# Queries and keys projected transposed and stored as the operands of the attention's scores

## The chip, the cores and the metric

The kernel runs on one core of a Trainium2 chip. The metric is the device time of one execution in microseconds (us); the time of a kernel is the median of its runs. The engines of the core are named as in the profile: PE (TensorE, matrix products; PEld is its weight load), DVE (VectorE), ACT (ScalarE), POOL (GpSimd) and SP (SyncE, which here does nothing but start transfers). Data lie in 128 partitions of SBUF; matrix products are accumulated in PSUM, which has eight banks of 128 x 512 fp32 values. All five engines take their instructions in order, each from its own queue, and wait for one another by semaphores.

## The reference

One layer of a hybrid decoder, in fp32, for a prompt of 1024 rows of width 1024 and for eight samples that each decode one token over a paged cache of 8192 tokens. What matters here is the first part, for the prompt:

```python
def rmsnorm(x, g):
    xf = x.astype(jnp.float32)
    y = xf * lax.rsqrt(jnp.mean(xf * xf, axis=-1, keepdims=True) + EPS)
    return (y * g.astype(jnp.float32)).astype(x.dtype)
...
    h = xn @ w_in
    q = h[..., O_Q:O_K].reshape(B, T, ATT_HEADS, ATT_HEAD_DIM)
    k = h[..., O_K:O_V].reshape(B, T, ATT_HEADS, ATT_HEAD_DIM)
    v = h[..., O_V:O_F].reshape(B, T, ATT_HEADS, ATT_HEAD_DIM)
    logf = jax.nn.log_sigmoid((h[..., O_F:O_U] + b_f).astype(jnp.float32))
    u = jax.nn.gelu(h[..., O_U:O_Z])
    z = rmsnorm(jax.nn.gelu(h[..., O_Z:]), g_sgu_v).reshape(B, T, SGU_HEADS, SGU_HEAD_DIM)
...
    s = jnp.einsum('bqhd,bkhd->bhqk', q, k).astype(jnp.float32) * (ATT_HEAD_DIM ** -0.5)
    s = s + (cq.astype(jnp.float32).transpose(0, 2, 1)[:, :, :, None]
             - ck.astype(jnp.float32).transpose(0, 2, 1)[:, :, None, :])
    s = jnp.where(kpos[None, :] <= qpos[:, None], s, -jnp.inf)
    p = jax.nn.softmax(s, axis=-1).astype(v.dtype)
    return jnp.einsum('bhqk,bkhd->bqhd', p, v)
```

There are eight heads of 64 columns; `cq` and `ck` are running sums of `logf` over the tokens. Queries, keys and values of the prompt are 512 columns each, and keys and values are outputs as well. The rest is a gating group beside the attention, an output projection, cross-attention into 256 memory tokens, a gated MLP with a convolution over the rows, and a final norm; the samples go through the same with their own caches.

## The kernel before

**Products.** A large product is fp32 made of three products of halves: an operand is split into a high part (an fp32r copy, on ACT) and a low part (what is left, on DVE or POOL; `split`, L212), and `gemm3` (L246) adds high by high, high by low and low by high in PSUM. 1/rms of a row is not multiplied into x. It is put on at the evacuation of PSUM, as a scale of one value to a partition (`rstd`; for queries `rstd8`, an eighth of it), since a partition of the result is a token.

**Buffers.** U are 18 buffers of 128 x 1024, of which x transposed takes 16 (high and low, 8 blocks each) during the projections; T2 are seven of 128 x 520; KV four of 128 x 2048 (the cache's tiles and the rows of x); `wr`, `wh`, `wl` are four, five and four buffers of a weight piece as loaded, its high and its low part. PSUM has four banks `ba`, two `bb`, one `ms`, one `dv`; `BK()` takes `ba` and `bb` in turn, two to one.

**What sets the order.** The kernel is written as generators. The prompt's main one runs through the stages and yields an estimate of its PE time at many points; a driver (L1640 to L1660) then lets the background, the samples' decode over the paged cache, take a step whenever enough has gathered (`PACE`). The framework fixes the order of instructions on each engine and the slots of the buffers when the kernel is built, with the order in the program as priority; on the chip each engine follows its order, and an instruction waits for what it reads and for the slot that it writes. Transfers of SP and ACT share eight semaphore lanes that go round; a transfer also waits for the one that had its lane before.

**The projections, `p1` (L309 to L537).** Column groups in the order queries, forget logits with u, keys, values, z; 9 to 278 us of the profiled execution. For each group four pieces of `w_in` are loaded and split (`loaded`), and the samples' own small products are made from the unsplit weights (`sample_mm`, L262; summed by `sample_sum`, L276). Then for each of eight blocks of 128 tokens the block of x is the stationary operand and 512 columns of weights move (`mm_chunk`, and `by_rows` at L402 to L404 for four blocks at once, which lets the first products start as the pieces come in): eight blocks of the contraction by three products, 24 matmuls of 128 x 512. `evac` (L389 to L393) puts each result through ACT with its scale into a T2 buffer and stores it from ACT's queue: queries to a scratch `q_d`, keys and values to the outputs `o_k` and `o_v`, all with a token to a row. `stats` (L331 to L342), called for each half of 512 rows, loads the rows of x by SP behind all pieces of x transposed (`x_in`), sums their squares on ACT (L207), and makes 1/rms on DVE (L200), POOL (L201) and DVE (L341, L342).

**The attention (L638 to L828), once for each half of 512 query rows.** It goes over four pairs of heads, in each over two blocks of 256 rows, two heads and two blocks of 128 rows. `load` fetches the pair's queries, keys and values (three transfers from SP, L644 to L651). `setup` transposes queries and keys on PE (L657, L680), four blocks to a bank, and writes the operands of the scores: for each head `qq`, which has the high part of the queries in partitions 0 to 63 and the low part in 64 to 127 (copies L663, L664 on ACT, subtract L665 on DVE); `ka`, the high part of the keys twice, one above the other (L684 on ACT; L688 on ACT in the first half, L686 on POOL in the second); `kb`, the low part (L689 on DVE). Four rows of the running sums are loaded beside them from POOL's queue. With these, two matmuls give the scores of a block in full accuracy (`scores`, L704 and L706), to which a causal mask is added on the diagonal. DVE takes the maximum (L709), ACT the exponential (L714); `turn` transposes the probabilities (L732) and ACT or DVE copies them (L739); `values` multiplies (L748); a closing step normalizes. Turns and values follow the scores two blocks behind. The next pair is loaded at the point `LD` and set up at the point `ST`, spread over yields, in the midst of the pair before. The memory's key and value projections (`pmem`) and, in the background, the decode's steps run among these.

## Time and profile before

| | |
|---|---|
| median of 3 runs | 1987.51 us (1987.01 to 1988.8) |
| the profiled execution | 1999.7 us, its span 1997.9 us |
| mean granted clock of PE | 0.958 |
| projections of queries | 9 to 60 us |
| forget logits with u | 60 to 118 us |
| keys | 118 to 175 us |
| values, then z | 175 to 278 us |
| attention of both halves | 278 to 545 us: PE busy 224.7 of 267, DVE 181.6, ACT 172.1, POOL 94.6, clock 0.91 |
| all that follows | 545 to 1998 us: PE busy 1352 of 1452 |

Busy times of an engine are given beside the length of the stretch, in us; a granted clock of 1.00 is the full one and 0.50 half. A line such as `PE ba L704 <- ACT u L688` means that PE, about to write a `ba` bank at line 704, waited for ACT to finish the tile `u` at line 688. Line numbers are those of the kernel before unless a text says otherwise.

### The profile page before, as it was taken

The page shows a single profiled execution, that of the slowest core. Times are in us where ns is not written, and L with a number is a line of the kernel's source. Part 1 is how long each engine was busy: PE and PEld are TensorE (multiplying, and loading weights), DVE is VectorE, ACT ScalarE, POOL GpSimd, SP SyncE. Part 2 cuts the span into 40 slices and gives each one's busy share as a digit, 9 for nine tenths or more (in the row PEclk, how much of TensorE's full clock was granted, in tenths as well). Part 3 has the DMA queues.
Part 4 walks back from the last instruction along what each step waited for, and adds up shares of the span by engine and source line. Part 5 has one row for each costly group of instructions (what it writes and reads, how often), then busy time and mean ns, then how long its engine had stood idle before and what let it go on. Part 6 is the DMA issues. An engine that isn't in the chain of part 4 may idle for free.

```text
span 1997.9 us, 24107 instructions
## 1 busy us (share of the span) xinstructions
PE 1838.5 (92%) x9159; PEld 1300.7 (65%) x9159; DVE 1332.5 (67%) x1467; ACT 732.9 (37%) x1344; POOL 988.4 (49%) x560
## 2 busy tenths in 40 slices
PE   8899989778999697999999999789999999899997
PEld 5777766556667455676777667566566668567773
DVE  3877456677677988998879999885424439532232
ACT  5332246566632322332323323322424423232331
POOL 1664343433387547676767576557243344233321
PEclk9999989889999898899999999899999999899999
DMA  8766786754497888888878889878664458666755
GB/s 322 258 235 229 270 318 229 251 172 154 165 356 263 306 296 311 297 309 312 313 279 329 292 296 336 328 259 306 259 225 162 141 192 268 239 197 224 258 204 191
DMA packets 160467, 517.05 MB, mean 259 GB/s; under 512 B 20168, under 2 KB 41928, under 8 KB 127584
## 3 DMA queue, kind: packets, MB, share of 16 engines
q0 software_dynamic: 38528, 270.88, 36.3%
q1 hardware_dynamic: 114912, 232.06, 33.6%
q10 hardware_dynamic: 6912, 12.59, 1.7%
q8 instruction: 72, 1.18, 0.2%
q14 instruction: 43, 0.35, 0.1%
HBM read 493.63 MB, written 21.84 MB: 258 GB/s over the span
## 4 chain that ended last, share of the span: by engine, by line
PE 65%; DVE 18%; DMA 6%; issue 5%; ACT 3%; POOL 2%; SPq 0%; POOLq 0%; ACTq 0%; DVEq 0%
PE ba L250 11%; PE ba L252 11%; PE ba L251 11%; PE bb L250 5%; PE bb L251 5%; PE bb L252 5%; DVE kv L1191 4%; PE dv L1250 4%; DVE s L1195 4%; DMA kv<-cache_k,kidx 2%; POOL wl L216 1%; DVE kv L1414 1%; PE dv L1493 1%; DMA kv<-cache_v,kidx 1%; PE ba L1022 1%
## 5 line engine op out<-in xcount | busy, mean ns | idle before, releaser
L216 POOL TENSOR_TENSOR wl<-wr,wh 128x1024 fp32r<-128x1024 f32 (+1 forms) x184 | 450.0, 2456 | 358.5 <-PE ba L252 211.6
L215 ACT ACTIVATE wh<-wr 128x1024 fp32r<-128x1024 f32 (+2 forms) x220 | 228.1, 1042 | 398.9 <-PE ba L251 105.1
L1191 DVE TENSOR_TENSOR kv<-kv,d 128x2048 f32<-128x2048 f32 (+1 forms) x109 | 308.7, 2836 | 42.6 <-DMA kv<-cache_k,kidx 42.4
L1183 POOL DMA_INDIRECT kv<-cache_k,kidx x128 | 175.8, 1373 | 287.4 <-PE dv L1250 110.3
L1195 DVE TENSOR_REDUCE s<-kv 128x32 f32<-128x2048 f32 (+1 forms) x139 | 292.1, 2107 | 29.4 <-POOL kv L1191 28.2
L1244 POOL DMA_INDIRECT kv<-cache_v,kidx x128 | 184.5, 1441 | 206.7 <-PE dv L1250 96.5
L250 PE MATMUL ba<-wh,u 128*128 128x512 f32 (+1 forms) x674 | 261.9, 390 | 7.1 <-ACT u L215 6.0
L251 PE MATMUL ba<-wl,u 128*128 128x512 f32 (+1 forms) x674 | 258.5, 384 | 1.3 <-DVE wl L216 1.3
L252 PE MATMUL ba<-wh,u 128*128 128x512 f32 (+1 forms) x674 | 257.6, 383 | 0.0
L250 PE MATMUL ba<-u,wh 128*128 128x512 f32 x568 | 231.3, 408 | 0.6 <-DVE u L219 0.5
L252 PE MATMUL ba<-u,wl 128*128 128x512 f32 x568 | 227.2, 401 | 0.0
L251 PE MATMUL ba<-u,wh 128*128 128x512 f32 x568 | 227.2, 400 | 0.0
L250 PEld LDWEIGHTS ba<-wh,u 128*128 128x128 f32 x674 | 128.1, 190 | 52.3 <-issue 17.8
L252 PEld LDWEIGHTS ba<-wh,u 128*128 128x128 f32 x674 | 127.8, 190 | 33.1 <-issue 7.5
L251 PEld LDWEIGHTS ba<-wl,u 128*128 128x128 f32 x674 | 128.2, 190 | 31.7 <-issue 6.5
L1250 PE MATMUL dv<-kv,s 128*32 128x512 f32 x1024 | 137.6, 627 | 5.5 <-DMA kv<-cache_v,kidx 5.5
L250 PEld LDWEIGHTS ba<-u,wh 128*128 128x128 f32 x568 | 108.9, 192 | 49.2 <-issue 14.3
L1191 POOL TENSOR_TENSOR kv<-kv,d 128x2048 f32<-128x2048 f32 (+1 forms) x30 | 117.0, 3908 | 43.9 <-DMA kv<-cache_k,kidx 38.7
L252 PEld LDWEIGHTS ba<-u,wl 128*128 128x128 f32 x568 | 108.5, 191 | 32.8 <-issue 7.6
L251 PEld LDWEIGHTS ba<-u,wh 128*128 128x128 f32 x568 | 108.7, 191 | 31.0 <-issue 5.9
L250 PE MATMUL bb<-wh,u 128*128 128x512 f32 (+1 forms) x318 | 125.5, 395 | 3.1 <-ACT u L215 1.5
L251 PE MATMUL bb<-wl,u 128*128 128x512 f32 (+1 forms) x318 | 123.3, 388 | 2.1 <-DVE wl L216 2.1
(395 smaller groups left out, 3079.1 us busy)
## 6 DMA issues: line engine op xcount, KB each, us to landing
wr<-w_up SPq DMA_DIRECT2D x88, 512.0 KB
kv<-w_up SPq DMA_DIRECT2D x22, 1024.0 KB
wr<-w_down SPq DMA_DIRECT2D x40, 512.0 KB
kv<-w_down SPq DMA_DIRECT2D x11, 1024.0 KB
wr<-w_in SPq DMA_DIRECT2D x16, 512.0 KB
wr<-w_o SPq DMA_DIRECT2D x16, 512.0 KB
wr<-w_cq SPq DMA_DIRECT2D x16, 512.0 KB
wr<-w_co SPq DMA_DIRECT2D x16, 512.0 KB
```

The costliest lines, as they stand in the source:

```text
L215: nc.scalar.activation(h, src, AF.Copy)
L216: (eng or nc.vector).tensor_tensor(l, src, h.bitcast(F32), op=ALU.subtract)
L250: mmul(out, sh, mh, start=(i == 0), stop=False)
L251: mmul(out, sh, ml, start=False, stop=False)
L252: mmul(out, sl, mh, start=False, stop=(i == n - 1))
L1022: mmul(ps, mv[:, mt, dd * P : (dd + 1) * P], pT[:, mt, :], start=(mt == 0), stop=(mt == 1))
L1183: nc.gpsimd.indirect_dma_start(kv, None, a["cache_k"], off(kidx[:, b, ch : ch + 1]))
L1191: eng.tensor_tensor(kvv[:, i : i + m, :], kvv[:, i : i + m, :], qb.unsqueeze(1).broadcast_to((P, m, 512)), op=ALU.mult)
L1195: nc.vector.tensor_reduce(s[:, ch * 4 + i : ch * 4 + i + m, :].rearrange("p k h -> p (k h)"), kvv[:, i : i + m, :].rearrange("p k (h d) -> ...
L1244: nc.gpsimd.indirect_dma_start(kv, None, a["cache_v"], off(kidx[:, b, ch : ch + 1]))
L1250: mmul(dv[32 * j : 32 * j + 32, :], s[:, ch * 4 : ch * 4 + 4, :].rearrange("p k h -> p (k h)"), kvv[:, j, :], start=(ch == 0), stop=(ch == ...
L1414: nc.vector.tensor_tensor(kn, kn, qb[n].unsqueeze(1).broadcast_to((P, 2, 512)), op=ALU.mult)
```

## The change

In the projections of queries and keys the operands trade places: a block of 128 weight columns (two heads) is stationary and 512 tokens of x move, so that a result has a head's column to a partition and a token to a column. There are as many matmuls of the same size. Values, u, z and the forget logits stay as they were. 1/rms now lies along the columns, so `stats` spreads it: `dg` is the identity times the four columns of `rstd`, and a product with ones gives every partition the whole row, which ACT copies to `rrow`, a further U buffer (lines 341 to 350 of the changed kernel). The first projection, `by_cols`, does four column blocks of the first 512 tokens at once. `evac_T` multiplies by scale and `rrow` on DVE, splits the result (a copy on ACT, a subtract on DVE), and stores high and low part each to a scratch of shape 512 x 1024 from ACT's queue; keys are also stored, unsplit, from SP to the output, which is transposed now and turned on the host. In the attention, `setup` and its point `ST` are gone, and so are its five yields per pair; `load` fetches the operands as they are used, three pieces of queries and three of keys per head and one of values per pair, 13 transfers from SP in place of three, into buffers that are all taken at the point `LD`. In the first half values now lie in a T2 buffer.

```diff
+        rrow = U([P, 2, 512])
...
-            nc.vector.tensor_scalar(rstd8[:, c], r, 0.125, None, op0=ALU.mult)
+
+            dg = T2()
+            nc.vector.tensor_tensor(
+                dg.rearrange("p (i t) -> p i t", t=P),
+                ident.unsqueeze(1).broadcast_to((P, 4, P)),
+                r.unsqueeze(2).broadcast_to((P, 4, P)),
+                op=ALU.mult,
+            )
+            ps = BK()
+            mmul(ps, ones, dg, start=True, stop=True)
+            nc.scalar.activation(rrow[:, hf, :], ps, AF.Copy)
...
+        def evac_T(ps, hf, hp, scale, hi, lo, out=None):
+
+            c = slice(hf * 512, hf * 512 + 512)
+            rows = slice(hp * P, (hp + 1) * P)
+            t, h, l = T2(), T2(512, F32R), T2(512, F32R)
+            nc.vector.scalar_tensor_tensor(t, ps, scale, rrow[:, hf, :], op0=ALU.mult, op1=ALU.mult)
+            split(t, h, l)
+            nc.scalar.dma_start(hi[rows, c], h.bitcast(F32))
+            nc.scalar.dma_start(lo[rows, c], l.bitcast(F32))
+            if out is not None:
+                nc.sync.dma_start(out[rows, c], t)
+
+        def by_cols(hf, ws):
+
+            pss = [BK() for _ in range(4)]
+            c = slice(hf * 512, hf * 512 + 512)
+            for k in range(8):
+                wh, wl = ws[k // 2][0][:, k % 2, :], ws[k // 2][1][:, k % 2, :]
+                for i in range(4):
+                    cb = slice(i * P, (i + 1) * P)
+                    mmul(pss[i], wh[:, cb], xh[k][:, c], start=(k == 0), stop=False)
+                    mmul(pss[i], wh[:, cb], xl[k][:, c], start=False, stop=False)
+                    mmul(pss[i], wl[:, cb], xh[k][:, c], start=False, stop=(k == 7))
+                yield 2.6
+            return pss
+
...
-        pss = yield from by_rows(0, ws)
-        for tt in range(8):
-            ps = BK() if tt > 3 else pss[tt]
-            if tt > 3:
-                mm_chunk(tt, ws, ps, 0, 512)
+        def mm_cols(hf, hp, ws, out):
+            c, cb = slice(hf * 512, hf * 512 + 512), slice(hp * P, (hp + 1) * P)
+            gemm3(
+                out,
+                [(ws[k // 2][0][:, k % 2, cb], ws[k // 2][1][:, k % 2, cb], xh[k][:, c], xl[k][:, c]) for k in range(8)],
+            )
+
+        pss = yield from by_cols(0, ws)
+        for i in range(8):
+            ps = BK() if i > 3 else pss[i]
+            if i > 3:
+                mm_cols(1, i - 4, ws, ps)
                 yield 5.2
-            evac(ps, q_d, rstd8, tt)
+            evac_T(ps, i // 4, i % 4, 0.125, qh_d, ql_d)
...
-                mm_chunk(tt, ws, ps, 0, 512)
+                if c0 == O_K:
+                    mm_cols(tt // 4, tt % 4, ws, ps)
+                else:
+                    mm_chunk(tt, ws, ps, 0, 512)
...
-                evac(ps, dst, rstd, tt)
+                if c0 == O_K:
+                    evac_T(ps, tt // 4, tt % 4, 1.0, kh_d, kl_d, a["o_k"])
+                else:
+                    evac(ps, v_d, rstd, tt)
...
+            qc, kc = slice(hf * 512, (hf + 1) * 512), slice(0, nk * P)
             qab, ka, kb = [], [], []
             for j in range(2):
                 h = hp * 2 + j
-                rows = slice(64 * j, 64 * j + 64)
+                rows = slice(h * 64, h * 64 + 64)
                 qq = U([P, 2, 512], F32R)
...
+                nc.sync.dma_start(qq[0:64, 0, :].bitcast(F32), qh_d[rows, qc])
+                nc.sync.dma_start(qq[64:128, 0, :].bitcast(F32), ql_d[rows, qc])
+                nc.sync.dma_start(qq[0:64, 1, :].bitcast(F32), qh_d[rows, qc])
+                nc.gpsimd.dma_start(qq[64:68, 1, :], cq_d[h, :, qc])
...
+                nc.sync.dma_start(ka[j][0:64, :].bitcast(F32), kh_d[rows, kc])
+                nc.sync.dma_start(ka[j][64:128, :].bitcast(F32), kh_d[rows, kc])
+                nc.sync.dma_start(kb[j][0:64, :].bitcast(F32), kl_d[rows, kc])
+                nc.gpsimd.dma_start(kb[j][64:68, :], ck_d[h, :, kc])
+            vn = (T2() if hf == 0 else U([P, nk * P])).rearrange("p (i c) -> p i c", c=P)
+            nc.sync.dma_start(vn, v_d[: nk * P, cs].rearrange("(i p) c -> p i c", p=P))
+            return qab, ka, kb, vn
...
-        for _ in setup(0, *load(0)):
-            pass
-        nxt = None
+        raw = load(0)
...
-                        if hp < 3 and (blk, j, ii) == ST[hf]:
-                            nxt = setup(hp + 1, *raw)
-                        if nxt:
-                            next(nxt, None)
-                            yield 1
```

More of the change, by code (lines that the diff above doesn't have):

```diff
@@ L58 @@
 TV = (0.0, 0.25)
-KP = 2
 PW = 1
 LD = [(0, 1, 0), (0, 0, 0)]
-ST = [(0, 1, 1), (0, 1, 1)]
 KG = 1
@@ L74 @@
 LT = 3
-SB = 2
 KS = 2
@@ L179, in constants @@
         nc.sync.dma_start(ws00[:, 8:16], a["bs00"].broadcast_to((8, 8)))
-    q_d = dram.tile([T, AW], F32, tag="q_d", name="q_d")
-    k_d, v_d = a["o_k"], a["o_v"]
+    qh_d, ql_d, kh_d, kl_d = (dram.tile([AW, T], F32, tag=n_, name=n_) for n_ in ("qh_d", "ql_d", "kh_d", "kl_d"))
+    v_d = a["o_v"]
     sgu_d = dram.tile([T, AW], F32, tag="sgu_d", name="sgu_d")
@@ L311, in p1 @@
         rstd = const.tile([P, 8], F32, tag="rstd", name="rstd")
-        rstd8 = const.tile([P, 8], F32, tag="rstd8", name="rstd8")
         ssx = sm([P, 8], "ssx", 1)
@@ L469, in gate_rows @@
                     nc.sync.dma_start(ck_d[:, 2 + r_, s], ng)
-        for c0, dst in ((O_K, k_d), (O_V, v_d)):
+        for c0 in (O_K, O_V):
             ws, sps = loaded(c0, 512, [(0, 512)])
@@ L780, in drain @@
                 queue.pop(0)()
-        got = []
-        for _ in setup(0, *load(0)):
-            pass
-        nxt = None
+        raw = load(0)
         yield 2
         for hp in range(4):
-            for _ in nxt or ():
-                pass
-            qkv, nxt = got.pop(), None
+            qkv = raw
             if hp == at and late:
@@ L1663 @@
 _OUT = {
-    "o_y": (T, D), "o_ys": (NB, D), "o_k": (T, AW), "o_v": (T, AW), "o_lf": (T, NH), "o_mk": (NMEM, D), "o_mv": (NMEM, D),
+    "o_y": (T, D), "o_ys": (NB, D), "o_k": (AW, T), "o_v": (T, AW), "o_lf": (T, NH), "o_mk": (NMEM, D), "o_mv": (NMEM, D),
     "o_h": (P, 2 * NF, 2), "o_hs": (P, 2 * NF, 8), "o_ks": (NB, AW), "o_vs": (NB, AW), "o_lfs": (NB, NH), "o_zs": (NB, AW), "o_s1": (P, 2 * NF, 8),
@@ L1733 @@
         o["o_ys"].reshape(NB, 1, D),
-        o["o_k"].reshape(1, 1, T, NH, HD),
+        np.ascontiguousarray(o["o_k"].T).reshape(1, 1, T, NH, HD),
         o["o_v"].reshape(1, 1, T, NH, HD),
```

34 lines of the change are left out of this document (removed).

## The prediction, as put on record before the changed kernel was run

> **What bounds the kernel now.** I read, in this order: the page's head (busy times and the chain that ended last), the table of stretches by stage, the timeline of the start and of the passage into the attention, then the waits of PE and the groups of the lines that go.
>
> ```profile
> span 1997.9 us, 24107 instructions
> PE 1838.5 (92%) x9159; PEld 1300.7 (65%) x9159; DVE 1332.5 (67%) x1467; ACT 732.9 (37%) x1344; POOL 988.4 (49%) x560
> PE 65%; DVE 18%; DMA 6%; issue 5%; ACT 3%; POOL 2%; SPq 0%; POOLq 0%; ACTq 0%; DVEq 0%
> ```
>
> PE is the bound: 92% busy, 65% of the chain. So I count PE's time: matmuls removed, and idle time opened or closed. Stretch by stretch (after the bounds: stretch, then busy us and count of PE, PEld, DVE, ACT, POOL, then granted clock, DMA share, GB/s):
>
> ```profile
> 9.00:60.00 51.00, 51.00 (x212) 37.56 (x214) 20.53 (x44) 31.16 (x47) 8.03 (x9) 1.00 0.93 342
> 60.00:118.00 58.00, 52.97 (x428) 49.09 (x432) 51.12 (x29) 15.78 (x26) 43.67 (x16) 0.94 0.72 250
> 118.00:175.00 57.00, 52.63 (x241) 39.06 (x234) 49.03 (x41) 19.46 (x26) 27.34 (x12) 0.97 0.60 212
> 278.00:300.00 22.00, 12.98 (x48) 10.23 (x48) 10.63 (x19) 16.02 (x34) 8.34 (x7) 0.77 1.01 385
> 300.00:340.00 40.00, 37.02 (x197) 26.60 (x196) 25.68 (x39) 24.69 (x54) 14.47 (x13) 0.96 0.77 264
> 405.00:440.00 35.00, 30.14 (x179) 19.56 (x178) 25.53 (x55) 23.20 (x66) 8.69 (x10) 0.85 0.42 129
> ```
>
> In the query stage (9 to 60) PE never rests; in the forget stage (60 to 118) and the key stage (118 to 175) it loses 5.0 and 4.4 us beside a DVE that is 88% and 86% busy; at the passage (278 to 300) 9.0 us with DMA full; in the attention (300 to 545) 33 us in small pieces (3.0, 5.0, 6.9, 4.9, 7.3, 5.9 and 0.4 by stretch).
>
> **The start, the largest term.** In the changed program the order on PE is: the eight small sample matmuls, then the first ones-matmul that spreads `rstd` along the columns (line 349), and only behind it the first query matmul. That ones-matmul reads `dg`, which DVE makes from the first half's `rstd`. When that is ready, the timeline of before shows (start, duration, engine, line):
>
> ```profile
> 9.12 1.65 PE L402 MATMUL ba<-wh,u 128*128 128x512 f32 x3
> 30.61 1.06 ACT L207 ACTIVATE junk<-kv 128x1024 bf16<-128x1024 f32 x1 [1.30 <-DMA kv<-x]
> 34.59 1.06 ACT L207 ACTIVATE junk<-kv 128x1024 bf16<-128x1024 f32 x1 [1.66 <-DMA kv<-x]
> 36.96 0.17 DVE L200 TENSOR_SCALAR r4r<-ssx 128x4 f32<-128x4 f32 x1 [4.07 <-ACT junk L207]
> 38.17 1.07 POOL L201 TENSOR_TENSOR r4r<-r4r,mhalf 128x4 f32<-128x4 f32 x1
> 39.28 0.17 DVE L341 COPY rstd<-r4r 128x4 f32<-128x4 f32 x1 [2.15 <-POOL r4r L201]
> 274.98 0.39 PE L402 MATMUL ba<-wh,u 128*128 128x512 f32 x1
> ```
>
> The rows of x land behind all of x transposed (30.6, 34.6), ACT squares them, DVE, POOL and DVE make `rstd` at 39.4. Before, only the evacuation needed it (ACT's line 392 at 39.61), and PE had four tiles of room. Now PE itself waits: it starts near 39.4 + 0.7 (`dg`, priced by DVE's rows of 512 columns below) = 40 instead of 9.1, a hole of 31 us. The 192 query matmuls (as many as before) run 0.23 us apart (274.98, 275.20, 275.43), 44.2 us; before they took 50.5 (9.1 to 59.6), since the first ran 0.43 apart (10.99, 11.42, 11.85), sample matmuls lay among them and some waited shortly for x. With everything landed, up to 4 us of that comes back, and the x rows could land some 3 us earlier, as sample splits leave their buffers earlier: **+28** (+24 to +31). The second ones-matmul stands 28 matmuls later, 6.4 us by 0.23, for a `rstd` that follows the first by two squares each of two loads; 0 to 3 us, inside that range. PE has no other work in its order to fill the hole.
>
> **Forget stage, −5 (−7 to 0).** At 75 PE stands 3.75 us behind DVE, which is in a decode multiply, and then runs at half clock for 6.8 us (77.6 to 84.4), worth 3.4. Now decode's loads and multiplies, which do not wait for the projection, come forward in relation to PE.
>
> **Evacuations, +3 (0 to +6).** Each of 16 changes from one ACT pass to a DVE multiply, an ACT copy and a DVE subtract, and one store to two (for keys a third, on SP). DVE's nearest rows are line 387's multiply over 8x512 (0.74 us) and setup's 64x512 subtract (0.69 us): 16 x 1.4 = 22 us. For the queries it lies in a stretch where DVE has 30 us free; for the keys 8 x 1.4 = 11.2 meet 49.0 of 57, 60 in all: 3 over. PSUM's six rotating tiles cover a late evacuation by 24 x 0.23 = 5.5 us each, hence 0; the end is all of what is over, twice. Three T2 buffers per tile instead of one out of seven leave two tiles in flight. Stores add 6 MB, 15 us of DMA time at 400 GB/s, spread over 160 us with DMA at 0.6 to 0.72: nothing, else what is said under late loads. 24 more issues on ACT's and SP's queues at 0.33 us (line 393) do not delay PE unless a lane is occupied.
>
> **Passage, −6 (−12 to 0).** Setup of the first pair stands in line on ACT behind a weight split that waits for its load:
>
> ```profile
> 282.29 1.06 ACT L215 ACTIVATE wh<-wr 128x1024 fp32r<-128x1024 f32 x1 [4.36 <-DMA wr<-w_ck]
> 283.25 0.57 ACT L663 ACTIVATE u<-ba 64x512 fp32r<-64x512 f32 x1
> 285.44 0.48 PE L704 MATMUL ba<-u,u 128*128 128x128 f32 x1 [7.37 <-ACT u L688]
> ```
>
> The 7.37 and 1.02 us gaps, eight transposes (0.9) and half clock until 292.6 (about 3) make 12. But behind the first four score matmuls PE's order has memory-key matmuls that need the same load, in a full DMA; so I take half.
>
> **Attention: transposes, −8.** 80 at 0.11 us start to start (277.04 to 277.47 for four); 72 outside the passage = 7.9 us, all on PE.
>
> **Attention: copies, −5 (−15 to 0).** These go: ACT 16 x 0.593 + 16 x 0.582 + 24 x 0.592 + 8 x 0.592 = 37.7 us, DVE 16 x 0.689 + 24 x 0.688 = 27.5, POOL 16 x 0.609 = 9.7.
>
> ```profile
> PE ba L704 <- ACT wr L714: 7.4, 6, 2.7
> PE ba L704 <- DVE u L689: 4.0, 3, 2.4
> PE ba L704 <- DVE u L665: 3.6, 2, 2.7
> PE bb L732 <- ACT wr L714: 3.3, 2, 2.3
> ```
>
> (us in total, times, longest.) Only 4.0 + 3.6 = 7.6 us are waits for setup itself; the exponentials (7.4 + 3.3) are late partly because ACT copies stand before them. I take two thirds of 7.6, as decode, which PE also waits for, stays; the end is 7.6 plus most of 10.7.
>
> **Attention: new waits, +3 (0 to +12).** Eight pairs load 13 pieces instead of 3, 80 more issues at 0.37 to 0.44 us (lines 644 to 651), 32 us of SP's queue, which is idle most of the time; what stands behind a load that waits for its buffer are weight loads of the memory projections and of what follows. All buffers of the next pair are taken at the load point instead of part at setup. In the second half 2 + 7 + 7 of 18 U buffers are then held, leaving two for turned probabilities; in the first, values hold two of seven T2, and exponentials wait for the turn two blocks back. None of this is in the trace: low end nothing (slots are mostly released 50 to 110 PE instructions ahead of first use), high end 24 blocks at 0.5 us, the mean of small waits such as line 732's behind its exponential. 20 fewer yields shift one or two decode steps beyond the attention: nothing net.
>
> **Sum:** +28 −5 +3 −6 −8 −5 +3 = **+10**. The profiled execution took 1999.7 us (span 1997.9 and 1.8 around it), 12.2 above the median of 1987.5 (1987.0 to 1988.8); with it 2009.7, against the median 1997.5.
>
> **Rivals.**
>
> *The attention gives back more than the start takes* (faster). Place: 278 to 545. If scores, exponentials and turns flow because ACT and DVE lose 65 us, 20 of the 33 idle us go instead of 5, and the passage gives its full 12: 28 −5 +3 −12 −8 −20 +3 = −11, 1976. It decides once passage, transposes and copies give more than 29 together. For it: ACT is 66% busy in 405 to 440 and stands in several waits. Against: DVE is 73% busy there mostly with decode, and line 748's values, line 1250 and the exponentials remain one chain. Chance 0.22.
>
> *The loads come late* (more slower). The attention's loads grow from 8.2 to 18.4 MB in pieces of 64 partitions. At 400 GB/s the 10.2 MB are 26 us of DMA; in 278 to 545 DMA is free for some 110 us, but not in 278 to 340: 53 of 62 are taken. If half of each pair's load shows (13 pieces, 1.8 MB at 400 GB/s = 4.5 us, and 7 in the second half), it is 4 x 2.2 + 4 x 3.5 = 23: 2020. Against: loads are issued a pair ahead, some 30 us. Chance 0.13. The Trainium skill ("DMA: Bandwidth & Descriptors", Rules for kernel authors) speaks for this one: two transfers to disjoint partition halves serialize, one of 128 partitions is to be used. No run here shows it; by its table under Bandwidth (64 KB at 138 GB/s) an estimate for the 10.2 MB would be 74 us, still under the 110 us free.
>
> *A wash*: passage −10 and copies −11 make the sum 0, 1987.5. Chance 0.12.
>
> *The hole is not there*, because PE's neighbours make `rstd` far sooner: it needs x rows by 10 us, and DMA at 0.93 in this stretch excludes it; 0.01, with the faster ones (28 less: 1969).
>
> Forecast as summed: 0.52. **Range** 1974 to 2017: from the faster rival to short of the late loads; the likeliest alone 1991.5 to 2010. 0.2% (4 us) is about what a measurement tells from no change. Faster 0.23, same 0.12, slower 0.52 + 0.13 = 0.65.
>
> **What would show it.** PE idle from 9 to about 40, with the ones-matmul after it waiting for DVE; the last query matmul near 87; no 3.75 us gap in the forget stage; first scores within 5 us of the last projection; lines 657 to 689 gone and PE idle in the attention near 28. Wrong would be: PE busy before 30; waits for DMA ahead of scores; key stage over 63 us; PE idle in the attention under 15 or above 45.

## The result, and the profile after

The changed kernel took 2015.3 us (median of 4 runs, 2012.4 to 2016.6) against 1988.2 us of the kernel before beside it; the ratio on record is 1.0118 with an interval of 1.0072 to 1.0165 (it is not the quotient of the two medians, which is 1.0137). On another chip, with more runs of both, it was 1.0072 (1.0041 to 1.0104). So it is slower by some 14 to 24 us. The median of the kernel before differs from one set of runs to the next (1988.2, 1996.5, 2001.3, 1994.2 and 1996.7 us), which is why kernels are compared below by the ratio to the runs of before that were made beside them.

The head of the page of the changed kernel:

```profile
span 2014.7 us, 24057 instructions
PE 1831.1 (91%) x9083; PEld 1291.1 (64%) x9083; DVE 1329.0 (66%) x1456; ACT 699.8 (35%) x1284; POOL 976.4 (48%) x543
PE 59%; DVE 19%; DMA 10%; issue 5%; POOL 3%; ACT 2%; SPq 0%; POOLq 0%; DVEq 0%; ACTq 0%
```

PE does 7 us less work, ACT 33 less, and the program is 17 us longer by its span: PE waits more, and in the chain that ended last DMA has grown from 6% to 10%. The start, on PE and on DVE (timelines, columns as before):

```profile
18.87 1.92 PE L260 MATMUL ba<-wr,xsT 128*32 128x512 f32 x4 [1.18 <-DMA wr<-w_in]
38.98 2.07 PE L349 MATMUL bb<-t,ones 128*128 128x512 f32 x2 [18.19 <-DVE t L342]
40.07 1.42 PE L423 MATMUL bb<-u,wh 128*128 128x512 f32 x1
```

```profile
38.17 0.17 DVE L339 COPY rstd<-r4r 128x4 f32<-128x4 f32 x1 [2.14 <-POOL r4r L199]
38.24 0.68 DVE L342 TENSOR_TENSOR t<-cp,r4r 128x512 f32<-128x512 f32 x1
```

PE waits 18.2 us for `dg` and starts the query projection at 40.1, as forecast to a tenth. Next, some stretches of the projections and the attention (stretch, then busy us of PE, PEld, DVE, ACT, POOL, granted clock, DMA share, GB/s):

```profile
306.00:328.00 22.00, 15.83 (x72) 12.45 (x70) 4.52 (x10) 9.96 (x23) 6.47 (x7) 0.84 1.03 339
328.00:368.00 40.00, 32.22 (x156) 22.14 (x156) 28.00 (x34) 18.14 (x39) 15.73 (x10) 0.87 0.82 293
405.00:435.00 30.00, 13.16 (x70) 11.36 (x70) 9.54 (x27) 4.47 (x14) 0.00 (x0) 0.66 0.77 194
435.00:470.00 35.00, 28.84 (x184) 19.45 (x184) 29.92 (x70) 24.59 (x77) 15.53 (x15) 0.95 0.90 272
470.00:505.00 35.00, 34.62 (x250) 23.41 (x249) 25.00 (x61) 22.61 (x70) 11.90 (x11) 1.00 0.81 218
```

The passage is better (15.8 of 22 busy against 13.0), the second half of the attention too (34.6 of 35 busy in 470 to 505, where no stretch of before but the last came so near), but from 405 to 435 PE stands idle for 17 us. PE's waits from 306 to 549 name the causes (us in total, times, longest):

```profile
PE ba L613 <- DVE u L605: 8.6, 1, 8.6
PE bb L756 <- ACT t L738: 8.5, 4, 5.3
PE bb L613 <- DVE u L605: 7.0, 1, 7.0
```

Lines 605 and 613 belong to the gating, which runs as filling work at the end of the first half. It had one such wait before, of 3.7 us. What its loads waited for, in SP's queue and on DVE:

```profile
SPq L592 <- DMA o_mv<-t: 11.5, 1, 11.5
```

```profile
404.25 0.35 SPq L592 DMA_DIRECT2D t<-g_sgu_v  x1
...
406.11 0.64 SPq L696 DMA_DIRECT2D u<-qh_d  x1
...
418.14 0.38 SPq L713 DMA_DIRECT2D u<-o_v  x1
419.36 0.36 SPq L602 DMA_DIRECT2D u<-zg_d  x1
```

```profile
428.05 1.42 DVE L605 SCALAR_TENSOR_TENSOR u<-u,rz,t 128x512 f32<-128x512 f32 x2 [8.82 <-DMA u<-zg_d]
```

The gating's first load waited 11.5 us for a store of the memory's values, whose T2 buffer and whose lane it needs. Its second pair of loads (419.36) stands behind the 13 operand loads of the second half's first pair (406.11 to 418.14), lands at 428, and PE waits with it.

The stage boundaries, read from the first or last matmul of each stage in each trace, with the span; the names of the kernels are those of the experiments below:

| kernel | forget stage starts | last matmul of the projections starts | attention ends | last decode matmul starts | span |
|---|---|---|---|---|---|
| before | 61.9 | 276.8 | 541.9 | 1527.9 | 1997.9 |
| before, again | 61.6 | 276.5 | 541.6 | 1526.4 | 1994.5 |
| b_hole | 90.7 | 305.1 | 566.9 | 1543.0 | 2011.8 |
| changed | 89.9 | 305.9 | 553.5 | 1553.7 | 2014.7 |
| changed, again | 90.9 | 301.2 | 551.8 | 1548.9 | 2010.0 |
| a_nohole | 83.7 | 298.6 | 555.6 | 1544.6 | 2007.3 |
| a_ms | 82.1 | 304.4 | 558.7 | 1548.8 | 2010.2 |
| a_yield | 88.6 | 304.1 | 551.0 | 1527.3 | 1997.1 |
| a_ghoist | 90.8 | 306.3 | 541.4 | 1548.7 | 2011.3 |
| k_only | 61.7 | 280.6 | 535.9 | 1514.1 | 1983.4 |
| b_noyield | 61.0 | 279.2 | 556.8 | 1553.1 | 2016.4 |
| a_nohole_yield | 82.9 | 298.7 | 557.4 | 1526.6 | 1995.5 |
| k_one | 61.5 | 284.0 | 605.6 | 1575.2 | 2044.3 |
| k_pace | 62.3 | 281.1 | 551.3 | 1506.1 | 1979.3 |

Two things are read from this table. From the last decode matmul to the end of the span it is 461 to 473 us in every row: a kernel whose decode ends later ends later by about as much. And the two executions of the changed kernel differ by up to 4.9 us at a boundary, so a difference of less than 5 us between two single profiles shows no effect by itself.

### The profile page after: what moved, and what is told of

The parts are those of the page before. It is cut to its first block, busy times and chain, and to the rows that moved or that the text cites. A ratio compares the mean times of both kernels' runs of the same rounds, so it can differ in the third digit from the quotient of the medians.

```text
span 2014.7 us, 24057 instructions
## 1 busy us (share of the span) xinstructions
PE 1831.1 (91%) x9083; PEld 1291.1 (64%) x9083; DVE 1329.0 (66%) x1456; ACT 699.8 (35%) x1284; POOL 976.4 (48%) x543
## 4 chain that ended last, share of the span: by engine, by line
PE 59%; DVE 19%; DMA 10%; issue 5%; POOL 3%; ACT 2%; SPq 0%; POOLq 0%; DVEq 0%; ACTq 0%
PE ba L248 10%; PE ba L250 9%; PE ba L249 9%; PE bb L248 5%; PE bb L249 5%; PE bb L250 5%; DVE kv L1205 4%; PE dv L1264 3%; DVE s L1209 3%; DMA kv<-cache_k,kidx 3%; POOL wl L214 2%; DMA wr<-w_o 2%; DVE u L214 2%; PE dv L1507 1%; DVE t L1083 1%
## 5 line engine op out<-in xcount | busy, mean ns | idle before, releaser
L1205 DVE TENSOR_TENSOR kv<-kv,d 128x2048 f32<-128x2048 f32 (+1 forms) x108 | 290.1, 2690 | 56.9 <-DMA kv<-cache_k,kidx 49.2
L1197 POOL DMA_INDIRECT kv<-cache_k,kidx x128 | 165.2, 1291 | 312.8 <-DVE s L1209 165.8
L248 PE MATMUL ba<-wh,u 128*128 128x512 f32 (+1 forms) x612 | 239.8, 394 | 10.8 <-ACT u L213 6.3
L248 PE MATMUL ba<-u,wh 128*128 128x512 f32 x616 | 247.7, 403 | 0.0
L250 PE MATMUL ba<-u,wl 128*128 128x512 f32 x616 | 244.9, 398 | 0.0
L249 PE MATMUL ba<-u,wh 128*128 128x512 f32 x616 | 244.2, 397 | 0.0
L249 PE MATMUL ba<-wl,u 128*128 128x512 f32 (+1 forms) x612 | 236.9, 388 | 6.8 <-DVE wl L214 5.3
L250 PE MATMUL ba<-wh,u 128*128 128x512 f32 (+1 forms) x612 | 235.4, 387 | 6.8 <-DVE u L214 6.8
L248 PEld LDWEIGHTS ba<-wh,u 128*128 128x128 f32 x612 | 118.7, 194 | 53.7 <-issue 18.0
L248 PEld LDWEIGHTS ba<-u,wh 128*128 128x128 f32 x616 | 117.1, 190 | 47.6 <-issue 15.9
L250 PEld LDWEIGHTS ba<-wh,u 128*128 128x128 f32 x612 | 118.1, 193 | 40.0 <-DVE u L214 9.3
L249 PEld LDWEIGHTS ba<-wl,u 128*128 128x128 f32 x612 | 118.6, 194 | 36.0 <-DVE wl L214 5.9
L249 PEld LDWEIGHTS ba<-u,wh 128*128 128x128 f32 x616 | 116.9, 190 | 32.6 <-issue 6.8
L248 PE MATMUL bb<-u,wh 128*128 128x512 f32 x312 | 125.6, 402 | 2.1 <-DVE t L408 2.1
L249 PE MATMUL bb<-u,wh 128*128 128x512 f32 x312 | 124.2, 398 | 0.0
```

The lines of the kernel that those rows point to most:

```text
L248: mmul(out, sh, mh, start=(i == 0), stop=False)
L249: mmul(out, sh, ml, start=False, stop=False)
L250: mmul(out, sl, mh, start=False, stop=(i == n - 1))
L1197: nc.gpsimd.indirect_dma_start(kv, None, a["cache_k"], off(kidx[:, b, ch : ch + 1]))
L1205: eng.tensor_tensor(kvv[:, i : i + m, :], kvv[:, i : i + m, :], qb.unsqueeze(1).broadcast_to((P, m, 512)), op=ALU.mult)
```

## The experiments

### The kernel before again: where its slower execution differs

No edit. 

> The kernel before once more, for a second profile of it, since the first one's execution (1999.7 us) lies 12 us above the median. If that surplus lay in one stretch, the stretches differ there and nowhere else; up to the end of the projections (277 us) I expect the same times within 1 us, and the surplus in the attention or later.

It took 1996.4 us in its set of runs, where 1996.5 was the median; its span of 1994.5 and its boundaries agree with the first profile within 1 us up to the attention's end and within 3.5 us after it. So the two profiles are alike, and stages may be compared with either; the surplus of the first one is not in one stretch.

### The hole alone

The kernel before, with `dg` and the product with ones put into `stats`:

```diff
             nc.vector.tensor_scalar(rstd8[:, c], r, 0.125, None, op0=ALU.mult)
+            dg = T2()
+            nc.vector.tensor_tensor(
+                dg.rearrange("p (i t) -> p i t", t=P),
+                ident.unsqueeze(1).broadcast_to((P, 4, P)),
+                r.unsqueeze(2).broadcast_to((P, 4, P)),
+                op=ALU.mult,
+            )
+            ps = BK()
+            mmul(ps, ones, dg, start=True, stop=True)
+            nc.scalar.activation(rrow[:, hf, :], ps, AF.Copy)
```

> The kernel before with only the hole: stats also builds dg, multiplies it with ones into a rotating PSUM tile and copies it to rrow, which nobody reads; queries and keys are projected and put away as before. Theory 1 (the start is the whole loss, and nothing later gives it back): PE waits from 21 to 39 us, and the time is that of the kernel before plus 27 (2012 to 2018). Rival (the start is mostly regained later, and the loss of the changed kernel comes from its attention): at most 12 us slower, below 2000.

The ratio is 1.0096 (1.0067 to 1.0125), 13 to 25 us. PE in its timeline:

```profile
18.88 1.92 PE L262 MATMUL ba<-wr,xsT 128*32 128x512 f32 x4 [1.31 <-DMA wr<-w_in]
38.87 2.08 PE L353 MATMUL bb<-t,ones 128*128 128x512 f32 x2 [18.07 <-DVE t L346]
```

The hole is the same to 0.1 us, with by-rows projections as with transposed ones: it comes from where the product with ones stands, not from the operands' trading places. It moves the forget stage by 29.1 us against the second profile of before, the attention's end by 25.3, the last decode matmul by 16.6 and the span by 17.3. Both theories were half right: the loss at its place is what I took, but about two fifths of it is regained, and not early: the difference is still 24 us at about 975 and 17 at 1450. What gives it back there was not pursued.

### The hole taken away

```diff
-            dg = T2()
-            ...
-            ps = BK()
-            mmul(ps, ones, dg, start=True, stop=True)
-            nc.scalar.activation(rrow[:, hf, :], ps, AF.Copy)
+        def spread(hf):
+            dg = T2()
+            ...
+            ps = MS()
+            mmul(ps, ones, dg, start=True, stop=True)
+            nc.scalar.activation(rrow[:, hf, :], ps, AF.Copy)
...
         pss = yield from by_cols(0, ws)
+        spread(0)
+        spread(1)
```

> The changed kernel without the hole: dg and the product with ones stand behind the first four column blocks and use the PSUM bank of its own (ms) in place of a rotating one. Theory 1: the first query matmul is back at 9 us, the query stage ends near 60, and the time is the changed kernel's less 26 (1983 to 1993), so about that of the kernel before. Rival (the start is regained later anyway): less than 12 faster than the changed kernel, above 2003.

The ratio to before is 1.0057 (1.0026 to 1.0088), to the changed kernel's 1.0118 and 1.0072 a gain of 3 to 12 us; the intervals overlap, so the gain is likely and not shown. PE starts at 9.1, but the forget stage still starts 21.8 us late. PE's waits in 60 to 90, and DVE there:

```profile
PE ba L260 <- DVE t L409: 11.0, 1, 11.0
PE ba L248 <- DVE t L409: 8.5, 1, 8.5
```

```profile
48.68 0.69 DVE L409 SCALAR_TENSOR_TENSOR t<-ba,u 128x512 f32<-128x512 f32 x1 [1.58 <-ACT u L351]
57.73 1.24 DVE L214 TENSOR_TENSOR wl<-wr,wh 128x1040 fp32r<-128x1040 f32 x1 [4.19 <-PE ba L250]
59.17 5.52 DVE L214 TENSOR_TENSOR wl<-wr,wh 128x1040 fp32r<-128x1040 f32 x1 [0.20 <-PE ba L250]
64.61 6.58 DVE L1208 TENSOR_TENSOR kv<-kv,d 128x2048 f32<-128x2048 f32 x1
74.00 0.66 DVE L409 SCALAR_TENSOR_TENSOR t<-ba,u 128x512 f32<-128x512 f32 x1
```

The first evacuation comes at 48.7, since `rrow`'s copy is late on ACT, and the fourth only at 74.0, behind weight splits and a decode multiply. Until then the rotating PSUM tiles are full and PE stands. So the hole has changed place: the results now need DVE, which the decode shares, where ACT took them before.

### One bank changed

```diff
-            ps = BK()
+            ps = MS()
             mmul(ps, ones, dg, start=True, stop=True)
```

> The changed kernel with one word changed: the two products with ones go into the bank ms, not a rotating one; they stay where they are in the program. PE's order then has 74 query matmuls and the samples' ahead of the first product with ones, some 18 us of work, so of the 31 us about 12 stay as a wait from 28 to 39. Theory 1: 15 to 20 us faster than the changed kernel (1995 to 2000). Rival: within 8 us of the changed kernel.

The ratio is 1.0088 (1.0059 to 1.0116), no clear gain over the changed kernel, although the forget stage starts 7.8 us earlier: in that stage PE stands 4.1 and 5.7 us behind query evacuations in DVE's queue, and keys start at 147.1 (148.4 in the changed kernel) and values at 202.0 (201.5). Theory 1 is wrong in its numbers here. What stays shown is the order's cause: with a bank of its own for the two products, 72 query matmuls (counted in the trace) and the samples' come ahead of them, so it was the rotation of the PSUM tiles that put the first one in front.

### The changed kernel on another chip

No edit. 

> The changed kernel once more, on the chip of the three that follow and beside the same runs of the kernel before, since its ratio so far (1.0118, interval 1.0072 to 1.0165) is too wide to compare single causes with. Expected: 1.010 to 1.014.

1.0072 (1.0041 to 1.0104): below what I expected, overlapping the first interval. Its span is 2010.0, 4.7 us less than that of the first profile, and it is ahead by 4.7 us already at the last matmul of the projections: the forget stage takes 53.7 us here and 58.6 there, at a granted clock of 1.00 and 0.91. So this stage differs between two executions of the same program by as much as several of the terms of the prediction.

### The yields put back

```diff
                             raw = load(hp + 1)
+                        if hp < 3 and (blk, j, ii) >= (0, 1, 1):
+                            yield 1
```

> The changed kernel with the yields of the removed setup put back as plain pacing: one yield of 1 at each of the five points of a pair, no work in them, so that the background gets its steps in the attention as before. Theory 2 (the attention's gain of 13 us, which the traces show between the kernel with the hole alone and the changed one, is lost at the end because the background's decode comes through late: sample work starts at 1577.8 instead of 1567.0): decode ends 8 to 11 us earlier and the time is 6 to 10 us below the changed kernel's. Rival (decode is late because of the buffers and loads of the attention, not of the pacing): within 3 us of the changed kernel.

The ratio is 0.9975 (0.9949 to 1.0001): beside the changed kernel on the same chip 1% or 19 us faster by the ratios and 14.5 us by the medians (2012.8 and 1998.2), about twice what I expected, with the hole still in it. Five yields per pair carry no work; they tell the driver how much time has passed, and the background gets its step. The last decode matmul (the group of line 1264, whose number is 1266 of the kernel with the yields; durations, then first and last start), first in the changed kernel, then with the yields:

```profile
L1264 PE MATMUL dv<-kv,s x1024: 591/593/1064, 245.5 to 1553.7; 128*32 128x512 f32 x171
```

```profile
L1266 PE MATMUL dv<-kv,s x1024: 589/592/1063, 243.7 to 1527.3; 128*32 128x512 f32 x171
```

Decode begins and PE reaches the attention within 2 us of the changed kernel, the attention ends 2.5 us earlier, but decode ends 26.4 us earlier, and the span is 17.6 us shorter. Beside the changed kernel's second profile it is 21.6 and 12.9 us.

### The yields taken from the kernel before

```diff
                             next(nxt, None)
-                            yield 1
+                            yield 0
```

> The kernel before with one number changed: the yields of 1 that go with the setup become yields of 0, so the setup still goes in the same pieces, but the background is paced as in the changed kernel; no instruction is added or removed. Theory 2 (30 units of pacing are worth some 20 us, since the background's decode, once late in the attention, stays late up to its end, and the end follows it): decode ends 15 to 25 us later and the time is 10 to 20 us above the kernel before (ratio 1.005 to 1.010). Rival (what the yields gave to the changed kernel was another order of its loads, not the pacing): within 4 us of the kernel before.

The ratio is 1.0107 (1.0073 to 1.0141), 15 to 28 us slower without an instruction more or less of the program's work. The same group of the kernel before, again, and without the yields:

```profile
L1250 PE MATMUL dv<-kv,s x1024: 592/593/1063, 209.8 to 1526.4; 128*32 128x512 f32 x171
```

```profile
L1250 PE MATMUL dv<-kv,s x1024: 592/592/1062, 212.5 to 1553.1; 128*32 128x512 f32 x171
```

Decode ends 26.7 us later, as in the changed kernel (22 to 27 us by its two profiles), and the span grows by 21.9. The two experiments agree: in these two pairs the yields are worth some 20 us by themselves, and the rival (that it was another order of loads) falls, since the loads here are those of the kernel before.

Where the time goes is less clear. Here 12.5 of the 21.9 us are lost within the attention already: it ends 15.2 us later, and the projections only 2.7. In the changed kernel the attention ends only 2.5 us later than with the yields. What both pairs share is the lag of the decode, and that it is not made up: of the 1024 matmuls of that group the 129th starts 52.6 us later than in the kernel before, again, the 193rd 26.7 us, the 513th 31.0 us and the last 26.7 us. In the changed kernel, against the one with the yields, the lag of every 64th from the 129th on lies between 8 and 36 us. From 800 to 1250 PE does less in both kernels without the yields (first the kernel before, again, and the same without the yields, then the changed kernel with the yields and the changed kernel):

```profile
800.00:1250.00 450.00, 441.88 (x2048) 314.34 (x2050) 398.48 (x318) 151.38 (x233) 312.13 (x171) 0.98 0.84 311
800.00:1250.00 450.00, 416.67 (x1922) 297.51 (x1919) 405.64 (x307) 143.60 (x220) 308.60 (x166) 0.96 0.81 298
800.00:1250.00 450.00, 438.08 (x2032) 312.58 (x2033) 412.02 (x322) 148.28 (x231) 311.03 (x171) 0.99 0.85 312
800.00:1250.00 450.00, 419.54 (x1911) 292.15 (x1910) 419.93 (x296) 141.34 (x213) 303.83 (x161) 0.97 0.80 294
```

With the yields PE is busy 442 and 438 of these 450 us, without them 417 and 420, while DVE is busy 398 to 420 in all four. In the attention of the kernel before DVE has room (182 of 269 us). So a decode step that leaves the attention comes where DVE has little room left. That this is why it is not made up is my reading; no run varies DVE's load there, and the pair without the hole (below) does not show it, with PE busy 431 us without and 432 with the yields.

### The gating's second loads moved ahead

```diff
+        zus = []
+        for pr_ in range(2):
+            z = U([P, 2, 512])
+            u = U([P, 2, 512])
+            rows = slice((hf * 4 + pr_ * 2) * P, (hf * 4 + pr_ * 2 + 2) * P)
+            nc.sync.dma_start(z, zg_d[rows, :].rearrange("(c p) d -> p c d", p=P))
+            nc.sync.dma_start(u, sgu_d[rows, :].rearrange("(c p) d -> p c d", p=P))
+            zus.append((z, u))
         for pr_ in range(2):
-            z = U([P, 2, 512])
-            u = U([P, 2, 512])
-            ...
+            z, u = zus[pr_]
```

> The changed kernel with one thing moved: the gating loads both of its row pairs at its start, ahead of the second half's first attention loads on SP's queue, instead of the second pair behind those 13 transfers. Theory 3 (PE's 8.6 us wait at 421 is for the gating's second load, which stands behind the attention's): that wait shrinks below 2 us, the 7.0 us wait before it stays, and the half of the attention that follows starts 7 to 10 us earlier; at the end of the attention 5 to 10 us remain, at the end of the kernel less, 0 to 8, if decode sets it. Rival (the wait only changes place: the second half's first scores then wait for their own loads): the end of the attention moves by less than 3 us.

The 8.6 us wait is gone and the other stays:

```profile
PE bb L617 <- DVE u L609: 6.7, 1, 6.7
```

The attention ends at 541.4, in the changed kernel's two profiles at 553.5 and 551.8. The ratio is 1.0071 (1.0049 to 1.0093), that of the changed kernel beside it to a ten-thousandth: of the 10 to 12 us that PE gains in the attention nothing reaches the end, while decode's last matmul starts at 1548.7, as in the changed kernel's profile from the same set (1548.9). Theory 3 holds for the attention, and it shows that a gain of PE alone there is worth nothing as long as the decode is late.

### Keys only

Queries are projected and set up as before; keys as in the changed kernel, `rrow` is made behind the query stage, and the yields stay:

```diff
             evac(ps, q_d, rstd8, tt)
+        spread(0)
+        spread(1)
...
+                if c0 == O_K:
+                    mm_cols(tt // 4, tt % 4, ws, ps)
+                else:
+                    mm_chunk(tt, ws, ps, 0, 512)
...
-            nc.sync.dma_start(kn, k_d[: nk * P, cs].rearrange("(i p) c -> p i c", p=P))
+                nc.sync.dma_start(ka[j][0:64, :].bitcast(F32), kh_d[rows, kc])
+                nc.sync.dma_start(ka[j][64:128, :].bitcast(F32), kh_d[rows, kc])
+                nc.sync.dma_start(kb[j][0:64, :].bitcast(F32), kl_d[rows, kc])
```

> One part alone: keys are projected transposed, split and loaded as operands as in the changed kernel; queries stay as in the kernel before (by rows, scaled on ACT, transposed in setup), so that nothing waits for rrow at the start, which is made after the query stage in the bank ms; the setup's yields stay too. Theory 1 and 2 (hole and pacing are what costs; key copies and transposes are a gain): no gap at the start, key stage not longer than before (53 against 55 us in the changed kernel), passage 2 to 6 us shorter, attention 4 to 10 us shorter, in all 5 to 14 us faster than the kernel before (ratio 0.993 to 0.9975). Rival (loads in twice the bytes and the buffers taken early cost what the copies gave): ratio 0.998 to 1.005.

1982.8 us, the ratio 0.9918 (0.9892 to 0.9944): 11 to 22 us faster than the kernel before, more than expected, and the fastest kernel of this study whose interval lies clear of 1. Its decode:

```profile
L1280 PE MATMUL dv<-kv,s x1024: 592/592/1064, 213.9 to 1514.1; 128*32 128x512 f32 x171
```

The start is as before (61.7). The key stage takes 56.9 us against 55.6, the first score comes at 283.5 against 285.1 although the projections end 4.1 later, the attention takes 252.4 from first score to end against 256.5, and the decode ends 12.3 us earlier than in the kernel before, with the same pacing. The rival, that loads in twice the bytes eat the gain, falls for the keys.

### Yields and no hole together

Both edits above. 

> The changed kernel with the yields put back and without the hole (products with ones behind the first four column blocks, in the bank ms). If the two causes add: the ratio of the yields alone (0.9975) less what the hole was worth beside the changed kernel (0.15 to 0.6%), 0.992 to 0.996; projections end near 299, attention near 546, decode 6 to 9 us earlier than with the yields alone. Rival (with the decode back in its place, the start's loss is covered by it): 0.997 to 0.999.

The ratio is 1.0023 (0.9999 to 1.0047), above what either expected. By the traces the two kernels end alike: last decode matmul 1526.6 and 1527.3, span 1995.5 and 1997.1, though the forget stage starts 5.7 us earlier without the hole. The causes do not add. With the decode in its place, the hole at the start is worth nothing that these runs could show when what replaces it is the wait for evacuations; why the ratio is half a per cent higher, beside other runs of before, stays open. The attention ends at 557.4, where 546 was expected.

This run also gives a third pair for the yields: beside the kernel without the hole they bring the ratio from 1.0057 to 1.0023, 7 us with overlapping intervals, the last decode matmul 18.0 us forward and the span down by 11.8. So the 20 us of the other two pairs are not a fixed price.

### One load for two halves

In the keys-only kernel:

```diff
-                nc.sync.dma_start(ka[j][0:64, :].bitcast(F32), kh_d[rows, kc])
-                nc.sync.dma_start(ka[j][64:128, :].bitcast(F32), kh_d[rows, kc])
+                nc.sync.dma_start(
+                    ka[j].bitcast(F32), kh_d[rows, kc].unsqueeze(0).broadcast_to((2, 64, nk * P))
+                )
```

> The keys-only kernel with each head's two loads of the keys' high part (64 partitions each, same source) replaced by one of 128 partitions with a repeated source: 5 and 7 transfers per pair become fewer by two, the bytes stay. If halves of the partitions cost a transfer of their own, the loads land earlier and the attention shortens by 2 to 6 us (ratio 0.989 to 0.991); if they are hidden a pair ahead, as the traces of the changed kernel let me think: within 2 us of the keys-only kernel (0.991 to 0.993).

2047.6 us, 1.0264 (1.0232 to 1.0295): neither theory; 3.5% slower than the keys-only kernel. PE waits for the queries' loads, and SP's queue shows why they are late:

```profile
PE ba L709 <- DMA t<-q_d: 39.3, 3, 21.6
```

```profile
414.48 0.52 SPq L697 DMA_DIRECT2D u<-kh_d  x1
416.79 12.15 SPq L685 DMA_DIRECT2D t<-q_d  x1
429.03 0.47 SPq L700 DMA_DIRECT2D u<-kl_d  x1
429.60 11.36 SPq L703 DMA_DIRECT2D u<-o_v  x1
```

Behind the loads with a repeated source transfers take long to be issued: of SP's 82 transfers from 280 to 606, 20 take over 2 us, up to 21.6, where in the keys-only kernel 2 of 115 do, and most take 0.4 to 0.5. The DMA share is 0.48 from 400 to 560 (0.73 in the keys-only kernel), and while such a transfer is held up it falls lower still: 0.14 from 437 to 441 and from 510 to 514, both at 53 GB/s. Two of the sixteen DMA engines alone would make a share of 0.125, and 512 KB at 53 GB/s take 9.9 us. That a load with two copies of its source runs on two engines is a reading; the trace does not number the engines. The keys-only kernel has loads of 128 partitions too (those of the values, for one), and most are issued in 0.4 to 0.6 us there. So the repeated source, not the number of partitions, was measured. The Trainium skill ("DMA: Bandwidth & Descriptors", Rules for kernel authors) says that two transfers to halves of the partitions serialize and one of 128 is to be used; this run does not test that rule, since its one transfer is of another kind, and how the rule fares here stays open.

### More background in the attention

```diff
-PACE = {'p1': 7.5, 'att0': 20.0, 'mid0': 6.0, 'ffn0': 7.5, 'att1': 15.0, 'mid1': 6.0, 'ffn1': 8, 'rest': 4.0}
+PACE = {'p1': 7.5, 'att0': 17.0, 'mid0': 6.0, 'ffn0': 7.5, 'att1': 13.0, 'mid1': 6.0, 'ffn1': 8, 'rest': 4.0}
```

> The keys-only kernel with more of the background in the attention: a step at every 17 and 13 units of pacing in place of 20 and 15 (about one and a half steps earlier, the other way from what the changed kernel did). Theory 2 in its general form (the end follows the decode, so each step that comes earlier is worth some 10 us): another 5 to 12 us faster, ratio 0.986 to 0.989. Rival (the pacing stood where more of it costs the attention what it gives the end): 0.990 to 0.996.

The ratio is 0.9958 (0.9916 to 1.0000): no gain over keys only, as the rival had it. In the profiled execution decode does end 8.0 us earlier (1506.1) and the span is 4.1 shorter (1979.3), but its runs fall into two groups, five from 1978.9 to 1985.4 and five from 1995.6 to 2004.3. The attention ends 15.4 us later than in the keys-only kernel (551.3 against 535.9), as the rival said. Theory 2 in its general form, each step earlier is worth 10 us, does not hold: the whole interval lies above the 0.986 to 0.989 that it gave. What is shown is the loss when steps are taken away.

## Why the prediction was right and where it was wrong

The direction was right, and the time lies in the range (2015.3 in 1974 to 2017). The sum, +10, was below the 14 to 24 measured. Of its terms the start was too large for the end, and the yields, put at nothing, cost the most. That the time lies in the range is partly luck: it is 1.7 us below the upper end, which had been set for late loads of the scores, and these did not occur.

**The start, +28: right at its place, too large for the end.** PE started at 40.1 and the forget stage moved by 28.0. At the end this hole is worth 17 of span and a ratio of 1.0096. The step took a shift of PE at 9 us to be a shift of the end, since PE is the bound; two fifths of it were regained behind the attention.

**The forget stage, −5: came in one profile of two.** In the first profile of the changed kernel a wait of 4.0 us is there still (at 90.3, for the low part of a weight piece, which DVE makes at 93.0 behind query evacuations and decode work), the clock granted in that stage is 0.91 against 0.94, and the stage takes 58.6 us against 57.5. In the second profile that wait is 1.7 us, the clock 1.00, and the stage takes 53.7 us. The prediction took a wait that comes and goes for a fixed one. (Before, PE's 3.75 us were for a copy on ACT, which waited for the forget logits on DVE, and these stood behind decode work.)

**Evacuations, +3: not contradicted beside the hole, too small without it.** The key stage takes 53.1 and 51.6 us in the two profiles, 50.9 in the kernel with the hole alone; that is less than two executions differ by. But the query evacuations were costed at nothing because DVE had 30 us free in that stretch; without the hole they cost PE 19.5 us (11.0 + 8.5), since they need `rrow` and stand behind splits and a decode multiply that POOL slows. The hole hid this in the changed kernel.

**Passage, transposes, copies and new waits, −6 −8 −5 +3 = −16: right in sum, in part by luck.** From the kernel with the hole alone to the changed one the attention's end comes 13.4 us earlier, to the one with the yields 15.9. The first score follows the start of the last projection matmul at 0.2 us (8.9 with the hole alone). But it is not made up as forecast, 8 us of transposes and 8 of waits. From the last matmul of the projections to the attention's end the kernel before, again, takes 265.1 us with PE busy 220.9, the changed kernel 247.6 with PE busy 205.9: PE is busy 15.0 us less, 10.2 of it the transposes and 4.9 the scores, whose matmuls take less time here, and its idle time fell by only 2.6. With the yields the stretch is 246.9 with PE busy 211.4, so that PE is busy 9.5 us less and idle 8.7 us less, nearer to the terms. Within it the new waits were larger than 3: the gating's two waits are 15.6 us against 3.7, and in the passage ACT stood 3.96 and then 2.18 us behind lanes that attention loads held, and PE waited 5.28 us from 313.6 on for an exponential that came behind them on ACT:

```profile
311.97 0.69 ACT L580 ACTIVATE t<-ba,rstd 128x512 f32<-128x512 f32 x1 [3.96 <-DMA u<-kl_d]
```

I had said that more issues cost nothing unless a lane is occupied; it was.

**"20 fewer yields shift one or two decode steps beyond the attention: nothing net": this step failed.** Taking the yields away costs 1.07% by itself in the kernel before, and putting them back gains 1% in the changed one, about 20 us each, and 7 us in the kernel without the hole. There are 30 yields of one unit, not 20; with a step at every 20 and 15 units in the two halves that is 1.75 steps, so the number of steps was right and its price was not. I had counted PE's time and named no price for the background. In the runs a step that leaves the attention is not caught up: decode ends 22 to 27 us later, and the end comes 461 to 473 us after it. Put in afterwards, this term at +18 and the start at +17, with −16 for the rest, make +19, inside the 14 to 24 measured. That is a sum fitted to the result and no proof, since the causes do not add where a run had two of them undone.

Of the rivals, late loads did occur, but for the gating, not for the scores, and moving them gave the end nothing. The faster rival had the place right, the attention, but a gain there could not pay without the yields.

## What to carry to other kernels

Where a background is paced by estimates that the main work yields, deleting work deletes pacing: keep the yields, or count the steps that move, before counting engine time. A scale that moves from the partitions to the columns needs its statistic as a row before the first evacuation, so change only the operands for which that row is long there: keys alone gave 0.9918, all of it 1.007 to 1.012. And look which engine's queue the new evacuation stands in, because a hole closed on PE may open again there.

## What the runs showed of the hardware that was not expected

DVE is held by POOL's multiplies of the same kind. In the kernel without the hole POOL shows two together from 58.96 on:

```profile
58.96 10.09 POOL L1208 TENSOR_TENSOR kv<-kv,d 128x2048 f32<-128x2048 f32 x2 [11.57 <-DMA d<-qs_d]
```

DVE's subtract over 128x1040 beside them took 5.52 us where the same took 1.24 just before, ending at 64.69, 1.1 us after the first of the two on POOL (63.59), and its multiply 6.58 us where it takes 2.28 alone (the one at 80.72), ending at 71.19, 2.1 us after POOL's end at 69.05. The Trainium skill ("SBUF — State Buffer", SBUF: two separate sides) states that the two engines share a pair of ports which one holds for its whole instruction while the other blocks; the trace agrees: each of the two on DVE ends about its own duration alone after one on POOL.

And loads whose source repeats along its outer dimension held up the issue of transfers behind them by up to 21.6 us, so that two transfers saved per pair of heads cost 3.5% of the kernel.
